# Convolution projections moved ahead of the retention's in a two-layer mixing kernel on one core

## The chip, the cores and the metric

The kernel runs on one core of one Trainium2 chip. The metric is the device time of one execution in microseconds (us). Three runs of the kernel before took 1466.75, 1464.87 and 1462.61 us; the median is 1464.87 us. Less is better.

## The reference

One inference step of two layers on 384 tokens: 128 of a prompt and 256 of a latent grid, which share all weights. All arrays are float32. Each layer does, on `h = x*(1+scale1)+shift1`:

```
mq,mk,mv,mo,mg, ca,cg, rq,rk,rv,rg, gm = split(h @ in_w)      # 1024 -> 8208 columns
y_a = (head_norm(mLSTM fwd + bwd of q,k,v,gates) * sigmoid(mo)) @ mlstm_out_w
y_b = silu(layer_norm(conv31(ca * sigmoid(cg)) + conv_b)) @ conv_out_w
y_c = (head_norm(retention fwd + bwd of rope(rq), rope(rk), rv) * silu(rg)) @ ret_out_w
x   = layer_norm(ALPHA*x + gate1 * ((sig(gm0)*y_a + sig(gm1)*y_b + sig(gm2)*y_c) @ out_w))
x   = layer_norm(ALPHA*x + gate2 * swiglu_ffn(x*(1+scale2)+shift2))
```

The mLSTM and the retention have four heads of 128 each, run in chunks of 128 tokens in both directions. `conv31` is a convolution of width 31 along the tokens, for each of 512 channels by itself. Outputs are both groups' tokens and the prompt's final states.

## The kernel before, in words

**Matmuls.** Every float32 matrix product is done as three fp32r products: weights and activations are split into a high and a low part, and `accum` (L253 to L261) issues hi*hi, lo*hi and hi*lo. A weight block comes from HBM into one of three buffers `wraw`, is cast on ScalarE (`whi`, L209) and its rest is taken on VectorE (`wlo`, L210). There are five buffers for high parts and four for low parts, of one column of 128 outputs each.

**Columns.** `colsA` (L281) does a projection of 512 outputs in four columns. A column of 1024 inputs is 24 matmuls of 384 tokens, one of 512 inputs is 12. After each column it calls an evacuation function, and then `tick` (L166) with weight 1 for 24 matmuls and 0.5 for 12. A tick advances every thread (a Python generator) by one step, and then issues `weight * rate["taps"]` taps of the convolution from the queue `dvq`. A thread that yields 1 skips the next tick. In layer 0 a tick also issues 0.3 steps of the modulation's matmuls (`adaps`, L377).

**The mixing stage** (`mixing`) runs the columns one after the other: gates, MQ, MK, RQ, RK, CG, CA, MO, RG, four each, and then three calls of `branch` (L854) for the mLSTM, the retention and the convolution. A branch has, twice, four columns of its gate (GM) and four half columns of its output matrix. Below, A, C and B stand for these three branches, and a pair such as GM C1 for the second gate block of branch C.

**What runs beside the columns.**
- The thread `heads` starts behind MK. It does the four mLSTM heads (`mheads`, L615) in 13 ticks, and then the four retention heads (`rheads`, L690) in two ticks each: decay tables `gef`, `geb` (L710 to L716), scores on TensorE (`sc1`, `sc2`), weighted scores on VectorE (`rpa`, `rpb`, L732 to L734), the products with the values (`rvo`, L737 to L743), and a norm (`headnorm`).
- `roped` (L752) turns the columns of RQ and RK: two ScalarE copies and four VectorE operations (L758 to L761) each.
- `put_u` (L767) makes the convolution's input from a column of CA, and queues its 31 taps. A tap is one VectorE instruction over 399 elements (L783; the first is L780, the last is the pair L786, which writes `xc`). Four columns have 124 taps.
- `gated` (L800) turns the normed heads and multiplies with `moT` or `rgT`; its result is `hA` or `hC`, two buffers each.
- `conv_norm` (L877) is a thread that starts with branch B. It turns `xc` on TensorE (L883) behind the first column of GM B0.

**Buffers.** Eleven buffers `m6` hold activations of four times 384 columns. During the retention heads eleven are held: four of `h1`, and `rv`, `haN`, `xc`, `rqT`, `rkT`, `moT`, `hcN`; `hA` (two) and `rgT` (one) need buffers of `rqT`, `rkT` or `rv`. Six buffers `w384` hold temporaries of 384 columns (`sig`, `gf`, `gef`, `geb`, `rpa`, `ropex`). Four hold `u` and `cacc`, so the fourth column's `u` waits until the first column's taps are through. There are eight PSUM tiles.

**Order.** A planner puts each engine's instructions into a fixed queue when the program is built: it takes those that it reckons ready by program order, blocks under `urgent()` 200 places earlier. On the chip each engine runs its queue in order.

Of the kernel before, what the change touches and what calls it, by code (L numbers as in the profile page):

```python
# [16 lines left out]
KT = 8  # L17
# [4 lines left out]
W = 512  # L22
# [7 lines left out]
KSC = 128.0 ** -0.5  # L30
# [3 lines left out]
M6 = 11  # L34
WRAW = 3
WADA = 1
TAPS1, TAPS2 = 2.0, 4.5
FILL = 0.3
LEADN = 4
AORD = {(0, 0): ((1, 1, 0, 16),), (0, 1): ((0, 1),), (0, 4): ((1, 2, 0, 16),), (0, 5): ((0, 2),),  # L40
# [9 lines left out]
O_RQ, O_RK, O_RV, O_RG, O_GM = 3088, 3600, 4112, 4624, 5136  # L50
# [49 lines left out]
def tile_kernel(ctx: ExitStack, tc: tile.TileContext, a: dict, o: list):  # L100
# [17 lines left out]
    def psum(name="ps"):  # L118
        return pp.tile([P, 512], F32, tag="ps", name=name)

    def m6(shape=(P, 4, T), dt=F32, name="m6"):
        return big.tile(list(shape), dt, tag="m6", name=name, bufs=M6)

    def tmp(shape, tag, bufs=2, dt=F32):
        n = 1
        for v in shape[1:]:
            n *= v
        if n in NB and bufs != 1:
            return sm.tile(list(shape), dt, tag=f"w{n}", name=tag, bufs=NB[n])
        return sm.tile(list(shape), dt, tag=tag, name=tag, bufs=bufs)  # L130
# [12 lines left out]
    def spawn(gen, delay=0):  # L143
        th = [delay, gen]
        threads.append(th)
        return th
# [19 lines left out]
    def tick(w=1.0):  # L166
        for th in list(threads):
            if th[0] > 0:
                th[0] -= 1
            else:  # L170
                step(th)
        rate["acc"] += w * rate["fill"]
        while rate["acc"] >= 1.0:
            rate["acc"] -= 1.0
            fill()
        rate["tacc"] += w * rate["taps"]
        n = int(rate["tacc"])
        rate["tacc"] -= n
        taps(n)
# [59 lines left out]
    def wcols(src, nk, ncols):  # L239

        cw = 1024 // nk
        for c0 in range(0, ncols, 512):
            n = min(512, ncols - c0)
            raws = []
            for k in range(0, nk, 4):
                raw = wp.tile([P, 4, n], F32, tag="wraw", name="wraw", bufs=WRAW)
                nc.sync.dma_start(raw, src[k * P:(k + 4) * P, c0:c0 + n].rearrange("(k p) f -> p k f", p=P))
                raws.append(raw)
            for q0 in range(0, n, 2 * cw):
                parts = [whl([P, nk, cw], *[r[:, :, q:q + cw] for r in raws]) for q in range(q0, min(n, q0 + 2 * cw), cw)]  # L250
                for hi, lo in parts:
                    for j in range(0, cw, P):
                        yield [(hi[:, k, j:j + P], lo[:, k, j:j + P]) for k in range(nk)]  # L253

    def accum(out, pairs, first=True, last=True):

        n = len(pairs)
        for i, ((sh, sl), (vh, vl)) in enumerate(pairs):
            mm(out, sh, vh, start=(first and i == 0), stop=False)  # L259
            mm(out, sh, vl, start=False, stop=False)  # L260
            mm(out, sl, vh, start=False, stop=(last and i == n - 1))  # L261
# [19 lines left out]
    def colsA(src, ncols, ha, nk, evac, first=0):  # L281

        for j, w in enumerate(wcols(src, nk, ncols)):
            ps = psum()
            accum(ps[:, 0:T], [(w[k], ha.part(k)) for k in range(nk)])
            evac(ps[:, 0:T], first + j)
            tick(nk / KT)
# [219 lines left out]
    def mixing(l, ha, v1, rv):  # L507
        inw = a["in_w"][l]
# [243 lines left out]
        def roped(dst, sc):  # L752
            def go(ps, j):
                xs = tmp((P, T), "ropex")
                act(xs[:, P:T], ps[:, P:T], AF.Copy, scale=sc)
                act(dst[:, j, 0:P], ps[:, 0:P], AF.Copy, scale=sc)
                sh = tmp((P, 256), "ropes")
                nc.vector.stream_shuffle(sh, xs[:, P:T], [i ^ 1 for i in range(32)])  # L758
                tt(sh, sh, sinE, op=ALU.mult)
                tt(dst[:, j, P:T], xs[:, P:T], cosE, op=ALU.mult)  # L760
                tt(dst[:, j, P:T], dst[:, j, P:T], sh, op=ALU.add)  # L761
            return go
# [60 lines left out]
        colsA(inw[:, O_MK:O_MK + W], W, ha, KT, lambda p_, j: act(mkT[:, j, :], p_, AF.Copy, scale=KSC))  # L823
        finish(thG)
        haN = m6((P, NT, NH, P), name="haN")
        rqT, rkT = m6(name="rqT"), m6(name="rkT")
        hc = []

        def heads():
            yield from mheads()  # L830
            yield from rheads()

        thH = spawn(heads())
        colsA(inw[:, O_RQ:O_RQ + W], W, ha, KT, roped(rqT, 1.0))
        colsA(inw[:, O_RK:O_RK + W], W, ha, KT, roped(rkT, KSC))
        xc = m6((P, NH, T), name="xc")
        rate["taps"] = TAPS1
        colsA(inw[:, O_CG:O_CG + W], W, ha, KT, put_sig)
        colsA(inw[:, O_CA:O_CA + W], W, ha, KT, put_u)
        moT = m6(name="moT")  # L840
        colsA(inw[:, O_MO:O_MO + W], W, ha, KT, put_mo)
        hA = Act(4, "hA")
# [125 lines left out]
    ha = Act(KT, "h1")  # L968
    inw = a["in_w"][0]
# [132 lines left out]
    aff = []  # L1102
    for l in range(DEPTH):
        mA = mixing(l, ha, v1, rv)
        while l == 0 and len(fillers) > 27:
            fill()
# [13 lines left out]
        for k0, n in ((0, 8), (8, 6), (14, 8)):  # L1120
# [8 lines left out]
            elif l + 1 < DEPTH:  # L1129
# [4 lines left out]
                ha = Act(KT, "h1")  # L1134
# [44 lines left out]
```

## Time and profile before

| | |
|---|---|
| median of three runs | 1464.87 us |
| the profiled execution | 1463.78 us |
| its span, first to last instruction | 1462.0 us |
| TensorE busy | 1424.2 us (97%) |
| VectorE busy | 933.0 us (64%) |
| ScalarE busy | 600.9 us (41%) |
| mean granted TensorE clock | 0.992 |

The profile is of one execution. PE is TensorE's matmuls, PEld its weight loads, DVE VectorE, ACT ScalarE, POOL GpSimd. A busy time counts an instruction from its start to its end. A matmul of 384 columns is listed with 0.33 us, though in a steady stretch one starts every 0.17 us, since they overlap. A wait names the instruction whose end released the waiting one.

### The profile page before, as it was taken

The page shows a single profiled execution, that of the slowest core. Times are in us where ns is not written, and L with a number is a line of the kernel's source. Part 1 is how long each engine was busy: PE and PEld are TensorE (multiplying, and loading weights), DVE is VectorE, ACT ScalarE, POOL GpSimd, SP SyncE. Part 2 cuts the span into 40 slices and gives each one's busy share as a digit, 9 for nine tenths or more (in the row PEclk, how much of TensorE's full clock was granted, in tenths as well). Part 3 has the DMA queues.
Part 4 walks back from the last instruction along what each step waited for, and adds up shares of the span by engine and source line. Part 5 has one row for each costly group of instructions (what it writes and reads, how often), then busy time and mean ns, then how long its engine had stood idle before and what let it go on. Part 6 is the DMA issues. An engine that isn't in the chain of part 4 may idle for free.

```text
span 1462.0 us, 20424 instructions
## 1 busy us (share of the span) xinstructions
PE 1424.2 (97%) x7990; PEld 1297.0 (89%) x7990; DVE 933.0 (64%) x1845; ACT 600.9 (41%) x1098; POOL 66.1 (5%) x102
## 2 busy tenths in 40 slices
PE   6999999999999999999999999999979999999997
PEld 4799999999987888989877999999979889898996
DVE  3456677998757644454374586887986666544447
ACT  2444677332525423323244356762325254242430
POOL 1000112000100000000010001100000000000000
PEclk8999999999999999999999999999999999999999
DMA  9565263564474565554655324244235426243441
GB/s 320 172 233 176 94 195 115 166 226 156 162 242 147 174 212 173 203 172 149 212 165 181 109 101 120 83 123 109 94 87 173 173 73 200 89 159 100 145 159 43
DMA packets 131712, 226.08 MB, mean 155 GB/s; under 512 B 12552, under 2 KB 62200, under 8 KB 126496
## 3 DMA queue, kind: packets, MB, share of 16 engines
q1 hardware_dynamic: 130144, 222.65, 46.3%
q0 software_dynamic: 1472, 2.14, 0.5%
q8 instruction: 62, 1.02, 0.3%
q14 instruction: 34, 0.28, 0.1%
HBM read 221.05 MB, written 3.71 MB: 154 GB/s over the span
## 4 chain that ended last, share of the span: by engine, by line
PE 77%; DVE 10%; DMA 8%; ACT 3%; issue 1%; POOL 1%; SPq 0%; DVEq 0%; POOLq 0%; ACTq 0%
PE ps L259 23%; PE ps L260 22%; PE ps L261 22%; DMA wraw<-in_in_w_dram 7%; DVE cacc L783 3%; DVE wlo L210 3%; PE adaps L377 2%; DMA adaq<-in_ada_w_dram 1%; ACT whi L209 1%; PE vacc L259 1%; PE vacc L261 1%; PE vacc L260 1%; PE adaps L1013 0%; POOL hrs L325 0%; PE ps L818 0%
## 5 line engine op out<-in xcount | busy, mean ns | idle before, releaser
L209 ACT CAST whi<-wraw 128x512 fp32r<-128x512 f32 (+1 forms) x484 | 338.0, 723 | 588.2 <-PE ps L260 249.3
L210 DVE TENSOR_TENSOR wlo<-wraw,whi 128x512 fp32r<-128x512 f32 (+1 forms) x484 | 384.6, 814 | 205.6 <-PE ps L261 98.9
L259 PE MATMUL ps<-h1h,whi 128*128 128x384 f32 x896 | 306.4, 342 | 0.0
L261 PE MATMUL ps<-h1h,wlo 128*128 128x384 f32 x896 | 300.7, 336 | 4.1 <-DVE wlo L210 4.1
L260 PE MATMUL ps<-h1l,whi 128*128 128x384 f32 x896 | 300.4, 335 | 0.0
L259 PE MATMUL ps<-h2h,whi 128*128 128x384 f32 x576 | 193.9, 337 | 0.0
L261 PE MATMUL ps<-h2h,wlo 128*128 128x384 f32 x576 | 192.6, 334 | 0.0
L260 PE MATMUL ps<-h2l,whi 128*128 128x384 f32 x576 | 192.6, 334 | 0.0
L259 PEld LDWEIGHTS ps<-h1h,whi 128*128 128x128 f32 x896 | 169.0, 189 | 13.7 <-issue 7.5
L261 PEld LDWEIGHTS ps<-h1h,wlo 128*128 128x128 f32 x896 | 168.9, 188 | 4.5 <-DVE wlo L210 4.5
L260 PEld LDWEIGHTS ps<-h1l,whi 128*128 128x128 f32 x896 | 168.9, 189 | 0.1
L783 DVE SCALAR_TENSOR_TENSOR cacc<-u,cwt,cacc 128x399 f32<-128x399 f32 x232 | 145.0, 630 | 2.7
L259 PEld LDWEIGHTS ps<-h2h,whi 128*128 128x128 f32 x576 | 108.1, 188 | 8.5 <-issue 5.0
L260 PEld LDWEIGHTS ps<-h2l,whi 128*128 128x128 f32 x576 | 108.1, 188 | 0.2
L261 PEld LDWEIGHTS ps<-h2h,wlo 128*128 128x128 f32 x576 | 108.1, 188 | 0.0
L259 PE MATMUL ps<-whi,fAh 128*128 128x512 f32 x264 | 103.4, 392 | 0.0
L261 PE MATMUL ps<-whi,fAl 128*128 128x512 f32 x264 | 102.9, 390 | 0.0
L260 PE MATMUL ps<-wlo,fAh 128*128 128x512 f32 x264 | 102.8, 389 | 0.0
L429 DVE TENSOR_TENSOR gmix<-ps,lnc 128x512 f32<-128x512 f32 x48 | 33.1, 689 | 84.9 <-PE ps L261 84.9
L955 DVE TENSOR_TENSOR gf<-ps,sig 128x384 f32<-128x384 f32 x36 | 20.1, 558 | 84.9 <-PE ps L261 84.8
L259 PEld LDWEIGHTS ps<-whi,fAh 128*128 128x128 f32 x264 | 49.5, 188 | 14.2 <-issue 4.2
L261 PEld LDWEIGHTS ps<-whi,fAl 128*128 128x128 f32 x264 | 49.5, 188 | 10.4
(307 smaller groups left out, 2011.6 us busy)
## 6 DMA issues: line engine op xcount, KB each, us to landing
wraw<-in_in_w_dram SPq DMA_DIRECT2D x64, 1024.0 KB
wada<-in_ada_w_dram SPq DMA_DIRECT2D x40, 1024.0 KB
wraw<-in_ffn_w_dram SPq DMA_DIRECT2D x76, 512.0 KB
wraw<-in_ffn_w_dram SPq DMA_DIRECT2D x28, 1024.0 KB
wraw<-in_out_w_dram SPq DMA_DIRECT2D x8, 1024.0 KB
adaq<-in_ada_w_dram SPq DMA_DIRECT2D x8, 512.0 KB
wraw<-in_mlstm_out_w_dram SPq DMA_DIRECT2D x4, 1024.0 KB
wraw<-in_ret_out_w_dram SPq DMA_DIRECT2D x4, 1024.0 KB
```

What stands on the lines that cost most here:

```text
L209: nc.scalar.copy(hi, src)
L210: tt(lo, src, hi.bitcast(F32), op=ALU.subtract)
L259: mm(out, sh, vh, start=(first and i == 0), stop=False)
L260: mm(out, sh, vl, start=False, stop=False)
L261: mm(out, sl, vh, start=False, stop=(last and i == n - 1))
L377: mm(st["ps"][32 * g:32 * g + 32, :], cs[:, k, :], wt[:, 512 * g:512 * g + 512], start=(k == 0), stop=(k == KT - 1))
L429: tt(g, ps, lc[0 if t == 0 else 1, hf], op=ALU.mult)
L783: tc.keep_in_program_order(stt(ac, u[:, k:k + CW], wk, ac, op0=ALU.mult, op1=ALU.add))
L955: tt(f, ps, sg[j], op=ALU.mult)
```

## The change

The four columns each of CG and CA come before those of RQ and RK. The retention's heads now begin only when the RK columns are issued: `heads` waits in a loop for `got`. The taps go out at 2.6 for a tick before the branches (2.0 before) and at 3.2 in the branches (4.5 before). The buffers `rqT` and `rkT` are taken after `xc`.

```diff
-TAPS1, TAPS2 = 2.0, 4.5
+TAPS1, TAPS2 = 2.6, 3.2
...
-        rqT, rkT = m6(name="rqT"), m6(name="rkT")
-        hc = []
+        hc, got = [], []
 
         def heads():
             yield from mheads()
+            while not got:
+                yield 0
             yield from rheads()
 
         thH = spawn(heads())
-        colsA(inw[:, O_RQ:O_RQ + W], W, ha, KT, roped(rqT, 1.0))
-        colsA(inw[:, O_RK:O_RK + W], W, ha, KT, roped(rkT, KSC))
         xc = m6((P, NH, T), name="xc")
         rate["taps"] = TAPS1
         colsA(inw[:, O_CG:O_CG + W], W, ha, KT, put_sig)
         colsA(inw[:, O_CA:O_CA + W], W, ha, KT, put_u)
+        rqT, rkT = m6(name="rqT"), m6(name="rkT")
+        colsA(inw[:, O_RQ:O_RQ + W], W, ha, KT, roped(rqT, 1.0))
+        colsA(inw[:, O_RK:O_RK + W], W, ha, KT, roped(rkT, KSC))
+        got.append(True)
         moT = m6(name="moT")
         colsA(inw[:, O_MO:O_MO + W], W, ha, KT, put_mo)
```

Counted in ticks behind MK (24 up to the branches), the program's order is:

| | before | after |
|---|---|---|
| mLSTM heads | 1 to 13 | 1 to 13 |
| RQ, RK (turning) | 1 to 8 | 9 to 16 |
| CG, CA | 9 to 16 | 1 to 8 |
| MO, RG | 17 to 24 | 17 to 24 |
| retention heads | 14 to 22 | 17 to 24, the last product behind tick 24 |
| taps up to the branches | 12 ticks of 2.0: 24 | 20 ticks of 2.6: 52 |
| taps in branches A and C (weight 24) | 100 at 4.5, over 22.2 | 72 at 3.2, over 22.5 |

## Rows read from the trace of the kernel before

**Rows 1.** The page, part 1: busy us (share of the span), instructions.
```profile
PE 1424.2 (97%) x7990; PEld 1297.0 (89%) x7990; DVE 933.0 (64%) x1845; ACT 600.9 (41%) x1098; POOL 66.1 (5%) x102
```
**Rows 2.** Waits of PE, whole span: releaser, us in total, times, longest.
```profile
PE ps L883 <- DVE xc L786: 5.8, 1, 5.8
PE ps L261 <- DVE wlo L210: 4.1, 1, 4.1
PE rvo L737 <- DVE rpa L732: 3.4, 3, 1.8
PE svo L659 <- DVE dl L647: 1.4, 1, 1.4
```
**Rows 3.** Windows: GM C0, C1, B0 of layer 1, and GM B0 of layer 0 (last).
```profile
core 0: us, PE busy (x) PEld busy (x) DVE busy (x) ACT busy (x) POOL busy (x), PEclk, DMA share, GB/s
1027.73:1044.37 16.64, 16.64 (x97) 16.64 (x97) 16.57 (x31) 2.82 (x4) 0.00 (x0) 1.00 0.29 97
1052.69:1075.32 22.63, 18.48 (x98) 18.16 (x97) 20.91 (x38) 3.48 (x5) 0.00 (x0) 0.92 0.20 52
1083.64:1110.25 26.61, 20.80 (x121) 20.50 (x121) 21.59 (x42) 12.10 (x22) 2.87 (x3) 0.94 0.37 126
366.46:386.23 19.77, 19.77 (x128) 19.67 (x125) 15.32 (x30) 8.62 (x15) 3.68 (x7) 1.00 0.64 214
```
**Rows 4.** Timeline of PE, layer 1: start, us, what, count [idle before <-releaser].
```profile
962.75 0.46 PE L737 MATMUL rvo<-rv,rpa 128*128 128x128 f32 x2 [1.84 <-DVE rpa L732]
...
1060.84 0.33 PE L261 MATMUL ps<-h1h,wlo 128*128 128x384 f32 x1
...
1065.67 0.44 PE L261 MATMUL ps<-h1h,wlo 128*128 128x384 f32 x1 [4.14 <-DVE wlo L210]
...
1066.45 0.52 PE L261 MATMUL ps<-h1h,wlo 128*128 128x384 f32 x1
...
1094.10 2.18 PE L883 MATMUL ps<-cc,xc 128*128 128x128 f32 x9 [5.80 <-DVE xc L786]
```
**Rows 5.** Waits of DVE, and of ACT, from 984 to 1094 us.
```profile
DVE wlo L210 <- ACT whi L209: 11.6, 3, 5.8
...
ACT whi L209 <- DMA wraw<-in_in_w_dram: 35.1, 7, 10.7
```
**Rows 6.** Windows by tap line L783: DVE busy with taps (count), layer 1 then 0.
```profile
900.69:976.34 75.65, 12.61 (x21) 0.98 0.34 100
976.34:1094.35 118.01, 59.70 (x96) 0.98 0.38 108
255.53:366.46 110.93, 60.83 (x97) 1.00 0.52 180
```
**Rows 7.** Windows, layer 1: RQ, CG, RG; last the sum of RQ to RG.
```profile
834.73:856.73 22.00, 22.00 (x142) 21.86 (x141) 16.54 (x50) 10.79 (x26) 0.00 (x0) 1.00 0.32 104
...
879.46:900.69 21.23, 21.23 (x134) 21.13 (x134) 12.37 (x40) 15.06 (x35) 2.42 (x4) 1.00 0.36 106
...
950.91:976.34 25.43, 23.59 (x140) 23.05 (x138) 19.31 (x49) 16.89 (x32) 3.21 (x4) 0.93 0.34 93
sum 141.61, PE 138.15 PEld 135.94 DVE 105.56 ACT 91.77 POOL 14.97; mean PE 23.03 PEld 22.66 DVE 17.59 ACT 15.29 POOL 2.50
```
**Rows 8.** Groups by line: count | busy us, mean ns of one | idle before.
```profile
L783 DVE SCALAR_TENSOR_TENSOR cacc<-u,cwt,cacc 128x399 f32<-128x399 f32 x232 | 145.0, 630 | 2.7
L758 DVE STREAM_SHUFFLE ropes<-ropex 128x256 f32<-128x256 f32 x16 | 7.1, 446 | 0.0
L759 DVE TENSOR_TENSOR ropes<-ropes,cc 128x256 f32<-128x256 f32 x16 | 6.7, 421 | 0.0
L761 DVE TENSOR_TENSOR rqT<-rqT,ropes 128x256 f32<-128x256 f32 x8 | 3.4, 422 | 0.1
```
**Rows 9.** Timeline of ACT, layer 1: a table load and what follows.
```profile
947.17 1.28 ACT L793 ACT_TABLE_LOAD   x1
948.47 0.49 ACT L793 ACTIVATE moT<-ps 128x384 f32<-128x384 f32 x1
```
**Rows 10.** Timeline of ACT, layer 1, and of DVE's weighted scores behind it.
```profile
961.06 0.62 ACT L209 CAST whi<-wraw 128x512 fp32r<-128x512 f32 x1 [2.63 <-DMA wraw<-in_in_w_dram]
...
962.33 0.28 DVE L732 TENSOR_TENSOR rpa<-sc,gef 128x128 f32<-128x128 f32 x1
```

## The prediction

> **What bounds the kernel now.** I read the busy times first: TensorE has 1424.2 us of a span of 1462.0 us [rows 1], so there are under 38 us in which it does nothing, and the change doesn't touch its work. What it can win or lose are TensorE's waits. The list of these waits came next [rows 2]: the two largest, 5.8 us for the last tap (`xc`) and 4.1 us for a low weight part (`wlo`), and then four waits for heads, 3.4 us in three for `rpa` and 1.4 us for `dl`. All are waits for VectorE. Then I cut the mixing stages at the columns' borders [rows 3]. The two large waits lie in layer 1, in GM C1 and GM B0. In GM C0, just before, VectorE is busy for 16.57 of 16.64 us: it has become the bound there. Layer 0 runs the same stages without such waits; its modulation steps lengthen TensorE's side.
>
> A wait costs more than itself. After the wait of 4.14 us the matmuls are listed with 0.52 us instead of 0.33 [rows 4], and the granted clock of that window is 0.92 [rows 3], so part of it ran at 1.2 GHz instead of 2.4. 0.08 of 22.63 us is 1.8 us.
>
> **The change part by part.** The sum is made against the profiled execution, 1463.78 us, which is its span and 1.8 us around it and 1.1 us under the median.
>
> 1. *Fewer taps in the branches (4.5 to 3.2).* GM C1 took 22.63 us where the same four columns take 16.64 in GM C0: 5.99 us. GM B0 took 26.61 us in layer 1 and 19.77 in layer 0: 6.84 us [rows 3]. Together 12.8 us, with the slower clock in it. Do they go? Program order puts 28 taps fewer behind the heads (100 to 72). 96 taps there took 59.70 us of VectorE [rows 6], 0.62 us each, so 28 are 17.4 us less. The last tap was 5.8 us late, and would be 11.6 us early. For it to stay late VectorE would have to lose that much elsewhere. It does stand idle 11.6 us in this stretch, behind ScalarE casts that wait for weight loads [rows 5]; these idle times I leave as they are. I take all 12.8 us. Ends: 12.8, and 0 if the loads get as much later as VectorE gets freer. Layer 0 has no wait to give.
>
> 2. *More taps beside the heads (24 to 52).* 28 x 0.62 = 17.4 us more VectorE work between MK and the branches, in each layer. In layer 1 VectorE has 105.56 of 141.61 us there [rows 7]; it gets 123, or 87%. No bound on the whole, but the stages differ. RQ stands in the place of CG, beside the same mLSTM heads. CG's place had 12.37 us of VectorE in 21.23 us [rows 7]. Four columns of turning add 4 x (0.446 + 0.421 + two of 0.422) = 6.8 us [rows 8], 10.4 taps add 6.5 us: 25.7 us in 21.2. RK is about full as well, by the same additions on fewer head steps. VectorE gets some 5 us behind there. That TensorE stands for it I don't believe: the weight parts have four buffers, four columns of some 4 to 5.5 us each with the heads, and in GM C0 it took a branch and a half of overload to use them up.
>
> 3. *The heads' own waits.* They come where VectorE's queue stands behind a weight load: at 961.06 ScalarE has waited 2.63 us for `wraw`, `rpa` starts at 962.33 [rows 10], and `rvo` has waited 1.84 us [rows 4]. Such waits are 4.8 us in four now [rows 2], and the clock was 0.93 in RG [rows 7], another 1.8 us: 6.6 us. With a fuller VectorE queue I expect more, not fewer. No row shows heads under this load. Ends: 6.6 us gained (all gone), and 25 us lost (below). I take twice the number of waits, four more of 1.2 us, 4.8 us lost, nearest to the rows.
>
> 4. *Retention heads three ticks later.* This costs TensorE nothing by itself; the same products move. Their stores on POOL and the load of `S0` on SP move with them, behind a point where the buffer is long free. But `rgT` and `hA` need buffers that the fourth head's scores and products free. These scores were at tick 21, behind the first column of RG; they are now at tick 24, behind the last. The RG columns wait in PSUM for three ticks more, and their gatings in the six `w384`. I count 0 for it in the likeliest case, since the planner can let GM A0's columns go ahead; the other end is the third rival.
>
> 5. *Order of loads.* RQ, RK, CG and CA load the same bytes in another order: 0, within 1 us either way.
>
> Sum: -12.8 + 4.8 = -8.0, so 1455.8 us for such an execution, and 1456.9 against the median: **1457 us**.
>
> A rule of the Trainium skill speaks against part 4. "ScalarE: Activation LUTs", section "What ACT_TABLE_LOAD costs", puts a change between functions of two sets at about 2.66 us, a load of 1.283 us and a drain of 1.38 us. The trace shows the load with 1.28 us, and the next activation 0.02 us behind its end [rows 9]; no drain is seen. An estimate by that page: some seven loads in RG with 1.38 us more each are 9.7 us of ScalarE more. By the trace they cost 1.28 us, and I go by that.
>
> **The rivals.**
>
> *Heads get smoother (gain).* If the fuller queue doesn't hurt and the four waits go with their slow clock, part 3 gives 6.6 instead of -4.8: 1464.9 - 12.8 - 6.6 = 1445 us. For it: CG and CA beside the first heads leave VectorE freer than RQ did (16.54 of 22.00 us [rows 7]). Against it: the waits come from late loads, which stay.
>
> *The lead isn't rebuilt (no change).* If VectorE reaches the branches some 10 us behind, by parts 2 and 4, and its idle times there remain, GM C1 or GM B0 keeps its wait: half of the 12.8 is won, 4.8 us lost: 1464.9 - 6.4 + 4.8 = 1463 us. For it: 11.6 us of idle VectorE in the branches [rows 5] come from loads. Against it: 17.4 us less work is more than that.
>
> *ScalarE fills RG (no change).* RG has 16.89 us of ScalarE in 25.43 [rows 7]; one head more in it and two table loads of 1.28 us [rows 9] make some 23 in 29, which hides. Were each of its some seven changes of table twice as long as the load that rows 9 show, it would be 32 us in 29, and about 6 us a layer with the waits behind it: 1457 + 12 = 1469 us. For it: the retention's exponentials now meet RG's sigmoids as well as MO's. Against it: the activation starts 0.02 us behind the load. The page named in part 4 stands for this case.
>
> *RG piles up (slower).* Place: ticks 21 to 26. Four RG columns hold PSUM tiles until `rgT` has a buffer, and the heads' scores and products need four of the other four. If TensorE has no tile for the next column, it stands through a head's chain, scores to `rpa` to `rvo`: without a column of 4.2 us to cover it, about 4.5 us, and 1.8 us for the clock. Two such waits a layer are 12.6 us, 25 us in both: 1464.9 - 12.8 + 25 = 1477 us. It decides from two full waits in each layer; one a layer gives 1464.7. For it: eleven of eleven buffers are held, and the four sigmoids and four gatings want eight `w384` where there are six. Against it: nothing in the trace of before shows TensorE waiting for a tile [rows 2], though eleven buffers were held then too, for a shorter time.
>
> The Trainium skill, "Perfetto Trace Analysis", section "Optimization Strategy", says that a gap which repeats on the engine that should be full can mean too few buffers for the next tile. That is what this rival would look like; the trace of before shows no repeated gap.
>
> **How the numbers follow.** Forecast (1450 to 1461): 0.53. Heads smoother (about 1445): 0.13. Lead not rebuilt (about 1463): 0.16. ScalarE fills RG (about 1469): 0.03. RG piles up (1465 to 1480): 0.15. A measurement of this kernel can tell about 0.3% from no change, 4.4 us: faster is under 1460.5, slower over 1469.3. Faster: nearly all of 0.53, 0.13, and a little of the third, 0.67 together. Slower: most of the last, and a half of the one before, 0.13. The same: 0.20. The likeliest case's own range is 1450 to 1461. The range for 8 in 10 goes to 1445 for the second case and to 1471 for the fourth.
>
> **What would show it.** Right: GM C1 and GM B0 of layer 1 take 16.6 and about 19.8 us, and the waits for `xc` and `wlo` are gone; VectorE in RQ and RK at 90% or more with no TensorE wait for `wlo` there; waits at `rvo` or `svo` of some 8 to 10 us together. Wrong: TensorE waits in RG or GM A0 of several us in both layers, with `rgT` written only behind the fourth head; or waits of TensorE in RQ and RK; or the wait for `xc` still there.

## The result and the profile after

The changed kernel takes 1474.28 us (median of five runs, 1471.35 to 1474.98). Its ratio to the kernel before is 1.0063, with a 95% interval of 1.0051 to 1.0075: slower by 0.63%. The forecast was 1457 us, and the range up to 1471 doesn't hold the time. A slow run of the kernel before, of 2871.71 us, is left out of the ratio. The profiled execution took 1474.28 us, with a span of 1472.5 us: 10.5 us more than before. Lines behind the changed ones are three higher than before (L883 is now L886).

The page, part 1, of the kernel after; it answers to [rows 1]. Nothing is to be seen in it: TensorE is busy for 1.2 us more in a span that is 10.5 longer.

```profile
PE 1425.4 (97%) x7990; PEld 1296.8 (88%) x7990; DVE 930.6 (63%) x1845; ACT 611.4 (42%) x1106; POOL 64.0 (4%) x102
```

The waits of PE, whole span, as [rows 2]. The waits for `xc` and for `wlo` in the branches are gone. `rvo` has 17.1 us where it had 3.4, and three waits are new.

```profile
PE rvo L737 <- DVE rpa L732: 17.1, 3, 8.4
...
PE ps L596 <- ACT rkT L756: 4.3, 1, 4.3
...
PE sc L590 <- ACT cns L748: 1.2, 1, 1.2
...
PE ps L804 <- ACT hcN L613: 0.4, 1, 0.4
PE svo L659 <- DVE dl L644: 0.2, 1, 0.2
```

Windows, columns as in [rows 3]. First GM C1 and GM B0 of layer 1; then RG of layer 0 and of layer 1; then RQ, RK and MO of layer 1.

```profile
1076.49:1093.13 16.64, 16.64 (x98) 16.64 (x98) 14.09 (x23) 3.61 (x5) 0.00 (x0) 1.00 0.55 117
1101.45:1120.75 19.30, 19.30 (x121) 19.23 (x121) 14.41 (x28) 9.55 (x16) 1.64 (x3) 1.00 0.48 164
227.32:266.59 39.27, 30.48 (x193) 29.29 (x191) 32.55 (x88) 30.55 (x53) 5.49 (x7) 0.91 0.38 120
960.10:1000.16 40.06, 30.18 (x189) 28.97 (x187) 31.80 (x80) 31.44 (x53) 4.85 (x6) 0.87 0.40 115
890.97:912.19 21.22, 21.22 (x133) 21.12 (x133) 19.04 (x56) 11.74 (x32) 2.50 (x3) 1.00 0.33 106
912.19:932.45 20.26, 20.02 (x126) 19.73 (x126) 19.49 (x61) 10.75 (x30) 2.56 (x3) 1.00 0.50 118
932.45:960.10 27.65, 23.36 (x135) 22.91 (x135) 22.61 (x59) 17.27 (x34) 0.45 (x1) 0.94 0.37 91
```

The branches give what was counted: 22.63 us became 16.64, 26.61 became 19.30. RG takes it back. It is 40.06 us in layer 1 where [rows 7] have 25.43. Some of this isn't loss, since the products of three retention heads now stand in RG, and not of one; but TensorE is busy for 30.18 of the 40.06, at a granted clock of 0.87. A sum over parts of the span, by the starts of the columns: from the end of MK to GM A0, 9.8 us more in layer 0 and 12.7 in layer 1; from GM A0 to the last half column, nothing in layer 0 and 13.3 less in layer 1; 1.2 more ahead of the first mixing stage, which the change doesn't touch. Together 10.4 of the 10.5.

PE's timeline around the stop in layer 1 shows where RG's time goes. The columns as in [rows 4].

```profile
983.96 0.38 PE L588 MATMUL sc<-rqT,rkT 128*128 128x128 f32 x2
...
985.94 0.70 PE L590 MATMUL sc<-rqT,rkT 128*128 128x256 f32 x2 [1.16 <-ACT cns L748]
987.00 0.55 PE L804 MATMUL ps<-cc,haN 128*128 128x128 f32 x3 [0.36 <-ACT hcN L613]
995.89 0.79 PE L737 MATMUL rvo<-rv,rpa 128*128 128x128 f32 x2 [8.35 <-DVE rpa L732]
```

These are the fourth head's scores, the last of two turned tiles for `hA` that VectorE hasn't read yet (the other is of 979.46 us), and then nothing for 8.35 us until the fourth head's products. The stop in layer 0 has 7.81 us before the same instruction. VectorE's timeline in that time (some rows left out) tells what `rpa` waited for.

```profile
981.78 0.41 DVE L710 TENSOR_SCALAR gef<-cc,lg 128x384 f32<-128x384 f32 x1
...
988.09 0.55 DVE L798 TENSOR_TENSOR rgT<-ps,sig 128x384 f32<-128x384 f32 x1
...
989.32 0.41 DVE L711 TENSOR_SCALAR geb<-cc,lg 128x384 f32<-128x384 f32 x1
...
990.19 0.55 DVE L798 TENSOR_TENSOR rgT<-ps,sig 128x384 f32<-128x384 f32 x1
...
992.68 0.41 DVE L734 TENSOR_TENSOR rpb<-sc,gef 128x256 f32<-128x256 f32 x1
...
994.02 0.55 DVE L798 TENSOR_TENSOR rgT<-ps,sig 128x384 f32<-128x384 f32 x1
...
995.03 0.61 DVE L806 SCALAR_TENSOR_TENSOR gf<-ps,pvec,moT 128x384 f32<-128x384 f32 x1
995.56 0.28 DVE L732 TENSOR_TENSOR rpa<-sc,gef 128x128 f32<-128x128 f32 x1
```

`gef` and `geb` stand side by side in the code and came 0.3 us apart for the heads before it (968.63 and 968.96 us); for this head they are 7.5 us apart. The first `rgT` is written at 988.09, 28 us after the beginning of RG and 4 us after the fourth head's scores began, which with the head's `qw` are the last to read `rqT` and `rkT`. Before, it was written at 963.52, 12.6 us after the beginning of RG. Until `rgT` has a buffer, the sigmoids (`sig`) and the gatings of `hA` (`gf`) keep their `w384`, and `geb` and `rpa` need such buffers too. By their starts three `sig` (969.82, 977.02, 982.81 us), two `gf` (970.45, 977.21) and `gef` make up the six; `geb` follows behind the first `rgT`, `rpa` behind the third. VectorE itself is busy nearly without a break from 988 us on, with five taps (3.1 us) among its work before `rpa`. That the buffers are the link is a reading of the order; the experiments test it.

The other new wait is at the beginning of MO in layer 1, first on ACT, then on PE.

```profile
940.27 0.62 ACT L209 CAST whi<-wraw 128x512 fp32r<-128x512 f32 x1 [6.61 <-DMA wraw<-in_in_w_dram]
```
```profile
941.39 0.33 PE L596 MATMUL ps<-cc,rkT 128*128 128x128 f32 x1 [4.29 <-ACT rkT L756]
```

The copy that writes `rkT` is queued behind a cast that waits for weights. These were issued at 923.65 and 924.72, on both sides of a store on POOL (`nst`, L688, at 924.29). Before, the loads of that time were issued at 904.56 and 905.16, the store at 913.75, and the next loads at 927.55.

### The profile page after: what moved, and what is told of

Its sections match the earlier page's. It is cut to its first block, busy times and chain, and to the rows that moved or that the text cites. A ratio compares the mean times of both kernels' runs of the same rounds, so it can differ in the third digit from the quotient of the medians.

```text
span 1472.5 us, 20443 instructions
## 1 busy us (share of the span) xinstructions
PE 1425.4 (97%) x7990; PEld 1296.8 (88%) x7990; DVE 930.6 (63%) x1845; ACT 611.4 (42%) x1106; POOL 64.0 (4%) x102
## 4 chain that ended last, share of the span: by engine, by line
PE 80%; DVE 8%; DMA 5%; ACT 4%; issue 1%; POOL 1%; SPq 0%; DVEq 0%; POOLq 0%; ACTq 0%
PE ps L259 24%; PE ps L260 24%; PE ps L261 24%; DMA wraw<-in_in_w_dram 4%; PE adaps L377 2%; DVE cacc L783 2%; DVE wlo L210 2%; DMA adaq<-in_ada_w_dram 1%; ACT whi L209 1%; PE vacc L259 1%; PE vacc L261 1%; PE vacc L260 1%; DVE dl L636 0%; PE adaps L1016 0%; ACT L797 0%
## 5 line engine op out<-in xcount | busy, mean ns | idle before, releaser
L783 DVE SCALAR_TENSOR_TENSOR cacc<-u,cwt,cacc 128x399 f32<-128x399 f32 x232 | 144.5, 628 | 2.0
L261 PEld LDWEIGHTS ps<-whi,fAl 128*128 128x128 f32 x264 | 49.5, 188 | 10.4
```

The lines of the kernel that those rows point to most:

```text
L783: tc.keep_in_program_order(stt(ac, u[:, k:k + CW], wk, ac, op0=ALU.mult, op1=ALU.add))
```

## The experiments

Ratios are to the kernel before on the same chip, with a 95% interval; each kernel was run in three rounds. The theory: in the new order `rgT` has no buffer until the fourth head frees one, and everything in RG piles up behind that. The rivals: more taps beside the heads fill VectorE; or the place of the gatings; and for the wait in MO, the taps or the store.

**The rates alone, in the old order.**

```diff
# the kernel before
-TAPS1, TAPS2 = 2.0, 4.5
+TAPS1, TAPS2 = 3.4, 3.7
```

> The order of before with even taps alone (3.4 beside the heads, 3.7 in the branches): 41 taps up to the branches instead of 24, 83 behind instead of 100. Theory (fewer taps in the branches cure layer 1; the loss of the change comes from the late retention heads): the waits in GM C1 and GM B0 of layer 1, 12.8 us with the slower clock, are gone or nearly; RG stays at about 24 to 26 us in both layers; 1452 to 1458 us. Rival (more taps beside the heads are what costs): RG or MO grow by 5 us or more in each layer and the time is 1465 us or more.

1458.22 us, ratio 0.9955 (0.9940 to 0.9970). RG, GM C0 and GM B0 of layer 1:

```profile
950.41:972.49 22.08, 21.98 (x139) 21.44 (x138) 15.02 (x36) 14.06 (x25) 2.31 (x3) 1.00 0.40 102
1024.17:1044.32 20.15, 17.52 (x97) 16.56 (x97) 18.55 (x33) 6.78 (x12) 0.00 (x0) 1.00 0.26 88
1077.61:1103.59 25.98, 21.80 (x122) 20.83 (x121) 20.85 (x40) 12.75 (x24) 1.64 (x3) 0.93 0.38 126
```

RG is shorter than in [rows 7], at a rate of 3.4 where the change has 2.6. More taps beside RG's heads are not what stops TensorE. The gain isn't where I expected it: by the starts of the columns 1.7 us (layer 0) and 4.7 us (layer 1) are won from the end of MK to GM A0, where `rvo` doesn't wait any more, while the branches lose 4.3 us in layer 0, 2.7 of them in one wait for weights of the modulation, and win only 2.8 in layer 1. GM C1 is cured (16.64 us), but GM C0 is 3.5 us longer than in [rows 3], and GM B0 is nearly as long as before.

**The order alone, with taps about as before.**

```diff
-TAPS1, TAPS2 = 2.6, 3.2
+TAPS1, TAPS2 = 1.2, 4.5
```

> The changed kernel's order of columns and late heads, with rates of 1.2 and 4.5, which leave about 24 and 100 taps as before. Theory (late heads): the stop before the last product of the fourth head at the end of RG stays, 7 us or more and a slower clock in both layers, though VectorE has 17 us less to do there; the waits in the branches of layer 1 return: 1478 to 1490 us. Rival (the load of the taps makes the stop): the stop falls to 2 us or less, RG is 25 to 28 us, and the time is 1464 to 1470 us.

1471.67 us, ratio 1.0044 (1.0029 to 1.0059): less slow than the theory had it, slower than the rival. The wait at `rvo`, and RG in layer 1:

```profile
PE rvo L737 <- DVE rpa L732: 10.6, 2, 5.3
```
```profile
948.08:984.39 36.31, 30.26 (x188) 29.39 (x187) 27.35 (x70) 29.46 (x48) 3.72 (x5) 0.91 0.44 127
```

The stop is there with as few taps as before, once in each layer; so the order makes it. But it is 5.3 us long and not 8; the five taps inside it in the changed kernel, 3.1 us of VectorE, come to about the difference. GM C1 lost its time again (20.99 us), as did GM B0 (26.15).

**One tick less for each retention head.** The first of the two steps in `rheads` is taken out, so the fourth head's scores come within MO, and its products behind RG's first column.

```diff
                     kws.append(kw)
-                yield 0
                 b1, b2 = scores(rkT, rqT, h)
```

> The changed kernel, but a retention head takes one tick instead of two (tables and scores in one step), so the fourth head's scores are at tick 20 and its products at tick 21, where they were in the kernel before. Theory (late heads): rqT, rkT and rv are free when RG begins, RG falls to 24 to 28 us, the branches keep no wait; 1452 to 1459 us. Rival (VectorE is too full with 52 taps and the heads in fewer ticks): waits for rpa of 2 us or more at several heads in MO, and 1465 us or more.

1456.69 us, ratio 0.9943 (0.9929 to 0.9958). Waits of PE, then MO and RG in layer 1:

```profile
PE ps L596 <- ACT rkT L755: 5.1, 2, 4.9
...
PE rvo L736 <- DVE rpa L731: 0.6, 1, 0.6
```
```profile
922.37:958.56 36.19, 31.28 (x192) 30.36 (x191) 30.27 (x86) 28.08 (x53) 3.99 (x5) 0.91 0.33 77
958.56:979.14 20.58, 20.58 (x132) 20.45 (x131) 14.97 (x42) 12.84 (x27) 3.48 (x4) 1.00 0.44 115
```

The stop is gone. MO and RG together are 56.8 us where they were 67.7. The fourth head's scores are now at 957.65 us, ahead of RG, and there is nothing to pile up.

**One buffer for `rgT`.** The retention's normed heads go into the mLSTM's value buffer, which is free by then, so that one `m6` more is there. Nothing else is edited.

```diff
-            hcN = m6((P, NT, NH, P), name="hcN")
+            hcN = sm.tile([P, NT, NH, 129], F32, tag="v1", name="hcN", bufs=1)[:, :, :, 0:P]
```

> The changed kernel, but hcN lies in the buffer of v1, which the mLSTM heads have just left, so that of the eleven m6 one is free for rgT when RG begins. No byte and no instruction more. Theory (rgT has no buffer until the fourth head's scores are through, and behind it the sigmoids, geb and PSUM tiles pile up): rgT is written within a column of its RG column, the stop before the fourth head's product falls from about 8 us to 2 us or less, RG from 39 and 40 us to 26 to 29 us in both layers; 1457 to 1463 us. Rival (late heads are long whatever the buffers, or hA's two buffers hold it up just as well): RG stays over 34 us, 1468 us or more.

1456.62 us, ratio 0.9933 (0.9917 to 0.9949): 17.7 us under the changed kernel, by one buffer. Waits of PE; RG in both layers; and the first `rgT` of layer 1:

```profile
PE rvo L737 <- DVE rpa L732: 5.3, 4, 2.4
PE ps L596 <- ACT rkT L756: 4.9, 1, 4.9
```
```profile
225.28:256.84 31.56, 28.82 (x192) 27.87 (x191) 26.39 (x77) 26.03 (x48) 5.46 (x7) 1.00 0.30 96
952.01:982.48 30.47, 28.02 (x189) 27.34 (x187) 23.88 (x64) 25.49 (x46) 4.17 (x6) 1.00 0.35 95
```
```profile
960.94 0.56 DVE L798 TENSOR_TENSOR rgT<-ps,sig 128x384 f32<-128x384 f32 x1 [0.43 <-ACT sig L797]
```

`rgT` is now written 8.9 us after the beginning of RG and not 28, and waits for its sigmoid and not for a buffer. `hA` still gets its buffers late (its first cast is at 981.43 us), so the buffer that counted is that of `rgT`. RG is 8 to 10 us shorter in each layer, and its clock is 1.00. Heads still wait 5.3 us in four at `rvo`, so RG stayed above what I expected.

**More room in the other pool.** `gef` and `geb` are taken from tiles of 512 columns, so that they ask for none of the six `w384`.

```diff
-                    ef, eb = tmp((P, T), "gef"), tmp((P, T), "geb")
+                    ef, eb = tmp((P, 512), "gef")[:, 0:T], tmp((P, 512), "geb")[:, 0:T]
```

> The changed kernel, but the decay tables gef and geb take buffers of 512 columns (three, unused in these ticks) instead of the six of 384. Theory (the fourth head's geb waits for one of six buffers that gated and sig hold, and these wait for rgT and hA): geb follows gef within 1 us, the stop before the last product shrinks from 8 us to 3 us or less in both layers, RG from about 40 to 33 us or less; 1458 to 1464 us. Rival (PSUM tiles held by the four RG columns are enough by themselves, or the chain of the fourth head is long anyway): the stop stays at 6 us or more, and the time at 1472 us or more.

1478.35 us, ratio 1.0099 (1.0081 to 1.0118): slower still, and not for the reason tested. Waits of PE, ACT's wait behind the first of them, and the GB/s of all DMA from 924 to 945 in 40 slices:

```profile
PE ps L596 <- ACT rkT L756: 13.9, 1, 13.9
PE ps L261 <- DVE wlo L210: 8.3, 3, 7.1
...
PE rvo L737 <- DVE rpa L732: 5.7, 2, 3.6
```
```profile
942.07 2.69 ACT L209 CAST whi<-wraw 128x512 fp32r<-128x512 f32 x5 [10.05 <-DMA wraw<-in_in_w_dram]
```
```profile
GB/s 0 0 0 8 31 12 16 0 4 8 12 47 12 12 12 16 4 16 16 4 4 4 8 23 160 179 133 203 281 328 363 371 328 347 363 289 179 137 82 27
```

The stop in RG did shrink, from 17.1 us in three to 5.7 in two; the temporaries are the second half of the chain. But the order of the queues shifted, and both weight loads were issued (925.02 and 925.69) right behind the store of `nst` (924.06). For 11 us hardly anything moves: some 10 GB/s; then the two loads pass at over 300. The wait that had 4.3 us has 13.9. The wait of 7.1 us for `wlo` is in layer 0, where the same happens: loads at 192.19 and 193.33 us, right behind the store at 191.79. This pointed at the store.

**The gatings of `hA` behind the heads.**

```diff
-        thA = spawn(gated(haN, moT, V_MN, hA))
...
-        finish(thA)
         finish(thH)
+        finish(spawn(gated(haN, moT, V_MN, hA)))
```

> The changed kernel, but the gating of the mLSTM heads is issued behind the retention heads, so that its four gf hold none of the six w384 and its turned tiles no PSUM in RG; rgT still has no buffer until late. Theory (rgT's buffer): RG's four columns still hold PSUM and sigmoids, but geb gets its w384: the stop before the fourth product falls to 2 to 5 us, RG to 29 to 34 us, some of it returns in GM A0 as the gating comes later; 1462 to 1470 us. Rival (the gating is harmless): stop of 7 us or more, 1473 us or more.

1464.61 us, ratio 0.9995 (0.9985 to 1.0005), as expected of the time and of the stops. Waits of PE:

```profile
PE rvo L737 <- DVE rpa L732: 4.7, 2, 3.7
PE rvo L737 <- ACT sig L797: 4.4, 1, 4.4
PE ps L596 <- ACT rkT L756: 3.9, 1, 3.9
```

9.7 of the 17.7 us, about half, go when the gating comes later. The edit takes the four `gf`, their turned tiles and their work on VectorE and ScalarE out of RG alike, so it doesn't show which of them counts; the rest, behind the sigmoids, stays. RG is still 36.3 and 34.0 us, longer than I expected.

**Two attempts on the store that did not reach it.** The first is the kernel with one tick less, with the store of `nst` behind the retention heads in program order; the second is the same with `hcN` in the free buffer as well.

```diff
-            nc.gpsimd.dma_start(new_n[0, l].rearrange("d h p -> p (d h)"), nst.rearrange("p d h -> p (d h)"))
+            nsts.append(nst)
...
+            nc.gpsimd.dma_start(new_n[0, l].rearrange("d h p -> p (d h)"), nsts[0].rearrange("p d h -> p (d h)"))
```

> e4_step, but the store of the mLSTM norms new_n (pieces of 4 bytes) is issued behind the retention heads instead of behind the mLSTM heads. Theory (this store meets the weight loads of MO at 925 us and slows them, which stops TensorE at the fourth column of RK, 4.9 us and a slower clock): that wait goes, MO of layer 1 takes 22 to 24 us, and the time is 4 to 7 us under e4_step, 1450 to 1453 us. Rival (the loads are late because VectorE frees the weight buffers late): the wait stays within 2 us of what it is, and the time within 2 us of e4_step.

> The three mends together on the changed kernel: one tick for a retention head, hcN in v1's buffer, new_n stored later. Theory: no stop of 2 us in RG, no wait at RK's end, the branches of layer 1 without waits: 1447 to 1452 us, the fastest so far. Rival (one tick a head makes VectorE the bound in MO once the other waits are gone): waits for rpa of 3 us or more in MO or RG, 1455 us or more.

1457.19 us (0.9943, 0.9928 to 0.9958) and 1456.76 us (0.9939, 0.9924 to 0.9954). The store was ready early, and the planner sent it early all the same: at 915.44 in the first, where it was sent at 914.22 without the edit. The wait at L596 stayed at 5.0 and 5.9 us. So these say nothing of the store, and that the second didn't come under 1452 says only that freeing the buffer adds nothing where the fourth head's scores are already through within MO.

**Fewer taps ahead of MO.** Both have `hcN` in the free buffer. The first has the rates 1.8 and 3.8; the second 2.0 up to RK and 3.3 from MO on.

```diff
-TAPS1, TAPS2 = 2.6, 3.2
+TAPS1, TAPS2 = 1.8, 3.8
```
```diff
-TAPS1, TAPS2 = 2.6, 3.2
+TAPS1, TAPS2 = 2.0, 3.3
...
         got.append(True)
+        rate["taps"] = TAPS2
```

> e5_v1 with rates of 1.8 and 3.8: 36 taps beside the heads instead of 52, 88 in the branches instead of 72. Theory (the wait at RK's end, 4.9 us and a slower clock in layer 1, comes from VectorE, 90 and 96% busy in RQ and RK, which frees the weight buffers late): RQ and RK of layer 1 fall under 85%, the wait goes, the branches keep a lead; 1449 to 1454 us. Rival (the wait comes from the loads' company on the DMA engines, whatever VectorE does): the wait stays within 2 us, 1455 us or more.

> e5_v1 with a rate of 2.0 from CA to RK and 3.3 from MO on. The same question with the taps held back only where the heads and the turning are: theory, the wait at RK's end falls to 2 us or less, but MO and RG get fuller and keep or raise their 5.3 us of waits for rpa; 1451 to 1457 us. Rival as for e9_r18: the wait stays, 1457 us or more.

1459.88 us (0.9960, 0.9946 to 0.9975) and 1459.60 us (0.9963, 0.9950 to 0.9976): neither better than 1456.62 with the change's own rates. The wait at L596 stays, at 2.8 and 4.5 us, though VectorE is busy for only 0.80 and 0.82 of RK (0.89 of RQ in both, more than I wanted); so fewer taps make it shorter, and VectorE isn't shown to make it. With 3.8 in the branches the wait for `xc` is back (4.9 us, GM B0 26.99); with more taps in MO and RG the heads wait more (6.8 us in six).

**The store moved for real.** To the kernel with the free buffer, a copy of `nst` is made on VectorE behind the retention heads, and the copy is stored.

```diff
-            nc.gpsimd.dma_start(new_n[0, l].rearrange("d h p -> p (d h)"), nst.rearrange("p d h -> p (d h)"))
+            nsts.append(nst)
...
+            nst2 = tmp((P, 2, NH), "nst2", 1)
+            tc.keep_in_program_order(nc.vector.tensor_copy(nst2, nsts[0]))
+            nc.gpsimd.dma_start(new_n[0, l].rearrange("d h p -> p (d h)"), nst2.rearrange("p d h -> p (d h)"))
```

> e5_v1, but the store of new_n now depends on a copy that VectorE makes in order behind the taps of the last retention head, so that it can't leave before. In e6_nst the planner had sent it at 915.44 us, as before (914.22 in e4_step), so that run told nothing of it. Theory (the store's 4 byte pieces slow the weight loads): the wait at RK's end goes from 4.9 us to 1 us or less, 1449 to 1452 us. Rival (late release by VectorE, or the load of S0 ahead of them): the wait stays over 3 us, 1455 us or more.

1452.82 us, ratio 0.9908 (0.9892 to 0.9925): the fastest, 3.8 us under the free buffer alone. The two intervals overlap by a little (0.9917 to 0.9949 there); the waits are what tells the two kernels apart. The same two weight loads are issued at 914.09 and 915.16 with the store between them (at 914.73), and at 913.77 and 914.84 without it. GB/s of all DMA from 914 to 930, in slices of 0.4 us, with the store and without:

```profile
GB/s 21 0 20 118 164 154 246 189 200 169 317 379 338 308 297 291 310 344 298 113 15 36 15 41 41 67 77 67 26 31 20 67 56 31 0 10 10 20 97 118
```
```profile
GB/s 0 0 87 164 200 241 215 174 164 210 328 379 323 307 312 282 317 307 364 302 200 169 159 56 5 10 10 0 0 0 0 0 0 0 0 0 0 20 0 0
```

And the last cast from these loads, with the store and without:

```profile
931.35 0.62 ACT L209 CAST whi<-wraw 128x512 fp32r<-128x512 f32 x1 [7.38 <-DMA wraw<-in_in_w_dram]
```
```profile
925.30 0.62 ACT L209 CAST whi<-wraw 128x512 fp32r<-128x512 f32 x1 [1.45 <-DMA wraw<-in_in_w_dram]
```

Both run alike until 921.6 us. Then the rest of the load trickles for some 9 us at some 40 GB/s where the store is about, and is through by 923.6 where it is not. A load of 16 KB of the program's instructions, on a queue of its own, is held up as well; the lines give MB and its share of 16 engines' time from 914 to 930, with the store (5.2 us) and without (0.9 us).

```profile
q8 instruction: 1, 0.02, 2.0%
```
```profile
q8 instruction: 1, 0.02, 0.4%
```

The load of `S0`, the rival, is issued ahead of both alike (910.38 and 910.05). The list of PE's waits has no L596 any more. MO and RG of layer 1 are 21.81 and 34.08 us, where they were 29.12 and 30.47 with the store: of 7.3 us won in MO RG gives 3.6 back, with waits of 6.7 us in five at `rvo` (5.3 in four) and a clock of 0.96; VectorE is busy for all of MO. That the heads wait because VectorE's queue comes fuller to RG is a reading of this.

```profile
922.58:944.39 21.81, 21.81 (x135) 21.43 (x135) 21.80 (x56) 16.47 (x31) 0.46 (x1) 1.00 0.33 104
944.39:978.47 34.08, 30.11 (x188) 28.87 (x187) 27.28 (x72) 29.11 (x54) 5.03 (x7) 0.96 0.35 96
```

**The free buffer in the old order.** The kernel before with the rates 3.4 and 3.7, and `hcN` in the mLSTM's value buffer as above.

> The order of before with rates of 3.4 and 3.7 (e1_rates) and hcN in v1's buffer. If a buffer for rgT is short in the old order too, RG gains a little: RG of both layers falls by 1 us or less, since the fourth head's scores come at RG's first column there anyway; 1456 to 1459 us, the same as e1_rates. If the buffers matter in the old order as they do in the new one, it is 1453 us or less.

1456.89 us, ratio 0.9937 (0.9922 to 0.9952). The interval overlaps that of the rates alone (0.9940 to 0.9970), and RG is 22.02 and 22.07 us in both layers. The buffer is not a gain by itself: it gains 17.7 us where the new order lacks it, and about nothing where it doesn't.

## Why the prediction was wrong

The step that failed is part 4: "I count 0 for it in the likeliest case, since the planner can let GM A0's columns go ahead". No column went ahead. RG's four columns, the two scores of the fourth head and two turned tiles for `hA` make eight PSUM tiles, as many as there are, and VectorE's next step needed a buffer. The first of them is read out with the first `rgT`, at 988.64 us, early in the stop (987.5 to 995.9), so the count alone doesn't explain all of it. From there on TensorE's queue had the fourth head's products ahead of GM A0's columns: in the trace they come first. Which of the two would have held the columns by itself isn't shown. That the missing buffer of `rgT` starts it is shown: with one more `m6`, and nothing else, 17.7 us went, and the first `rgT` came 8.9 us into RG instead of 28.

The rival "RG piles up" named the place and the buffers. Its form was off: I priced short waits of 4.5 us, two in each layer, and said that one in each would leave the time unchanged. There was one in each, of 7.81 and 8.35 us, and longer by itself than I had counted. The 4.5 us was a head's chain with free temporaries; here `geb`, the exponentials, `rgT` and taps stand in that chain as well (e.g. the 7.5 us from `gef` to `geb`). So its 1477 us was near the 1474.28, by a wrong count of waits. I gave it 0.15 because TensorE had never waited for a tile with eleven buffers held. That was the weak inference: before, the time for which they were held ended ahead of RG's last columns, and three ticks more carried it past.

The page "Perfetto Trace Analysis" of the Trainium skill, section "Optimization Strategy", says that a gap which repeats can mean too few buffers. Here the gap came once a layer, ahead of the same instruction, and the free buffer took both away: the trace agrees as to the cause. As a sign it was weak, since one gap in a layer is easily read as a slow VectorE, which is what the list of waits names.

*Part 1* was right: 5.99 and 7.31 us in GM C1 and GM B0, 13.3 over the branches of layer 1, against 12.8. The waits for `xc` and `wlo` there are gone, and they come back with 4.5 taps for a tick (GM C1 20.99, GM B0 26.15). One reading ahead of it was off: the two largest waits of the kernel before are not those two. A wait of 7.3 us for `x` comes first in its list; it isn't for VectorE, and it lies ahead of the mixing stages (6.7 us after).

*Part 2* was right in what it said of TensorE: VectorE is busy for 0.90 of RQ and 0.96 of RK, and there is no wait for `wlo` there; the one wait of TensorE in both is 0.2 us, at `svo`. Its sum for RQ, 25.7 us of VectorE in 21.2, was too high: 19.04 in 21.22 were measured.

*Part 3*: apart from the two stops, `rvo` and `svo` wait for 1.1 us (17.1 less 7.81 and 8.35, and 0.2), not for 8 to 10. Where the stops are gone they are 5.9 us in six (the free buffer), and 7.4 in seven with the store moved as well: more than the 4.8 in four of before, as I expected, and less than I counted. But a fuller queue of VectorE alone doesn't make them: with 41 taps in the old order (the rates alone) the heads wait for 1.1 us in one, and with the change's 52 and one tick less for a head for 1.6 in four.

*Part 5* was wrong: "0, within 1 us either way". The order brought two weight loads together with a store in small pieces: a wait of 4.3 us, and about 3.8 us of the time by the medians of the kernels with and without the store there. Part 4 named the stores on POOL as moved; the one that mattered, of `nst`, keeps its place behind the mLSTM heads (79.0 us after the end of MK before, 78.5 after), and it was the loads that moved onto it. I compared bytes and not the issue times of the queues.

ScalarE's table loads, which I weighed as a rival, were more (35 before, 43 after) and added their 1.28 us each to ScalarE: 600.9 became 611.4 us, eight more loads. With the free buffer there are 39. No wait of TensorE is shown to come from one of them alone.

All in all the part that I predicted to gain gained; with the buffer and the store mended, the new order takes 1452.82 us, below the forecast, and below the rates alone in the old order (0.9908 to 0.9955, intervals apart). Against the old order with the rates and the buffer (0.9937) the intervals meet.

That the order itself gains isn't shown. From the end of MK to GM A0 the mended kernel takes 288.8 us in the two layers together, the old order with the rates alone 279.3; what puts it ahead are the branches, 321.1 us against 335.7, where 72 taps are left and not 83. The old order with 52 taps ahead of the branches, some 4.3 for each of its 12 ticks, wasn't run.

## What to carry to other kernels

When a step moves later, list every buffer that it frees and who takes it next, pool by pool; a step can be free on every engine and still stop the kernel, if the buffer it frees is the last one that a full queue needs. A chain of waits that names an engine as busy can hide a buffer: look for two neighbouring instructions of the code that lie far apart in the trace, as `gef` and `geb` did. Before counting reordered transfers at nothing, set their new issue times beside those of small-piece stores on other queues.

## What was new of the hardware

A small store can cost more than a large one. DMA issues of the kernel after: size, median us from issue to landing.

```profile
out_dram<-cns POOLq DMA_DIRECT2D x16, 128.0 KB, 2.3
...
out_dram<-nst POOLq DMA_DIRECT2D x2, 4.0 KB, 12.4
```

The store of 4 KB is 1024 pieces of 4 bytes by its access pattern, and lands after 12.4 us, where 128 KB take 2.3 (in the kernel before 10.2 and 3.6). The Trainium skill, "DMA: Bandwidth & Descriptors", section "Specifications", puts the smallest transfer for full rate at 512 bytes. The trace agrees as to the store. The kernels with and without the store beside the weight loads show what it does to others: a 1 MB load that meets it is late by some 6 us (931.35 against 925.30). By what part of the DMA it is held up isn't shown; the load of instructions, on another queue, was held up too.

Stops cost clock as well. In layer 1 TensorE stood from 987.5 to 995.9 us, and the granted clock was 0.5 (1.2 GHz) from 989.4 to 999.7, so that 3.8 us of it lay behind the stop. In layer 0 it stood from 254.8 to 262.6, and the clock was 0.5 from 259.0 to 265.8, 3.2 us of it behind the stop. After the wait of 4.29 us in MO it was 0.5 from 941.6 to 945.1. Most of the fourth head's products in layer 1 fell into it: they are listed with 0.63 us, those of the third head with 0.39.
